# A two-layer encoder trunk: convolution matrices from DRAM, wide convolution, in-place layer norm, reordered start and last head

## The chip, the cores and the metric

The kernel runs on 1 core of one Trainium2 chip. The metric is the device time of one execution in microseconds; a measurement is the median of several runs.

## The reference

The input is x, 1024 frames of 1024 channels, float32. Two layers follow.

- Layer 0: RMS norm; one projection to 1536 columns. 512 "value" columns times the sigmoid of 512 "gate" columns go through a causal depthwise convolution of width 31, a layer norm over the 512 channels, and silu. The other 512 columns are pooled over 2, 4, 8 or 16 past frames, minus the frame itself, and mapped by one 128x128 matrix a group. Both halves are concatenated, projected to 1024 columns and added to x. Then RMS norm, an FFN `(silu(h w1) * (h w3)) w2` with 2816 hidden columns, added.
- Layer 1: RMS norm; a projection to q, f, i, g; a gated linear recurrence of 8 heads with a 128x128 state; head norm times silu(g); output projection, added. RMS norm and an FFN as above. A final RMS norm.

## The kernel before, in words

All activations are transposed: 128 channels by 512 frames is one tile, "half" 0 or 1 of the frames (NH = 2). Every large product is done with operands split into a high and a low part in fp32r, as three matmuls (lines 160 to 162): high times high, low times high, high times low. A weight tile of 128x1024 comes by one DMA on SP's queue into a raw tile (two of these, L141), is cast on ScalarE (L142) and its remainder is taken on VectorE (L143); there are three split tiles of each kind. The residual stream lies in DRAM (`hd`): `accumulate` copies a product out of PSUM into one of three `temp` tiles on ScalarE (L307) and adds it in DRAM by an accumulating DMA from POOL's queue (L308); `fetch` reads it back, also from POOL's queue (L312). `staged` takes a tile out of a pool of 72.

The order of each engine's queue comes from a scheduler that takes the ready instruction of highest priority; `tc.high_priority(offset=...)` lifts a block, `tc.issue_after` puts a block behind one instruction of its engine.

The start (L417 to 441) loads x in 16 tiles, squares it for the row norm (`squares`, ScalarE), transposes it on TensorE (L367), scales and splits it (`keep`), copies it for the residual (`hold`), and makes the first gated product (`glu`). The convolution of channel groups 0, 1 and 2 runs on VectorE, 31 taps of 128x512 each per group and half (`conv`, L470). Group 3 goes to TensorE as 36 products with banded 128x128 matrices (`conv_by_phase`); these matrices are built on GpSimd from a small table of taps and a diagonal (`conv_blocks`, L506), 8 at a time, and the results travel over DMAs (`cb<-cy`) to ScalarE (L539), which writes the group's `y`. Between them run the pooled columns: `project_u`, `map_u` (its copies `v` are L583), `mean_u` (L593), and the pooled half of the output projection (`op`). Then comes the layer norm, half 0 and half 1 (`mu`, `lss`, `ly`), and the convolved half of the output projection (`oa`) with its residual adds (L329).

In layer 1, `recur` is one head and half of the recurrence; it yields between its steps, and after each yield the loop takes that many steps (`BEFORE`) of a "filler": the projections of the next head (`project`: F, Q, values, and the gate G), then the output product of finished heads where `OUT_AT` says so (`ho`). One step is three matmuls of 512 columns, or as much. Behind the last head follows the rest of the output product with the residual (`h_ho`). An FFN starts with two column blocks done together, whose row norms are spread over the partitions by `rows`: a diagonal (`dg`, L200, VectorE) times ones on TensorE (`bc`).

Of the kernel before, what the change touches and what calls it, by code (L numbers as in the profile page):

```python
# [39 lines left out]
def trunk(ctx: ExitStack, tc: tile.TileContext, a, out):  # L40
# [94 lines left out]
    def load(src, shape, leng=None):  # L135
        uid[0] += 1
        i, n = uid[0], shape[0] * shape[1]
        raw = wpool.tile([P, 1024], F32, tag="wraw", name=f"wr{i}", bufs=NRAW)[:, :n]
        wh = wpool.tile([P, 1024], F32R, tag="wh", name=f"wh{i}", bufs=NSPLIT)[:, :n]
        wl = wpool.tile([P, 1024], F32R, tag="wl", name=f"wl{i}", bufs=NSPLIT)[:, :n]  # L140
        nc.sync.dma_start(out=raw.rearrange("p (a b) -> p a b", a=shape[0]), in_=src)  # L141
# [3 lines left out]
        return v(wh), v(wl)  # L145

    def cols(w, m0, nm=1, k0=0, nk=None):
# [3 lines left out]
    last_product = []  # L151
# [18 lines left out]
    def split(src, name, scale=None):  # L170
        hi, lo = act(f"{name}h"), act(f"{name}l")
        if scale is None:
            nc.scalar.copy(hi, src)
            nc.vector.tensor_tensor(lo, src, f32(hi), ALU.subtract)  # L174
        else:
            nc.scalar.activation(hi, src, AF.Copy, scale=scale)
# [14 lines left out]
    def broadcast(y, name, room, bank=mbank):  # L191
# [6 lines left out]
        for i, v in enumerate((f32(yh), yl)):  # L198
            dg = room(f"dg{i}_{name}").bitcast(F32R)
            nc.vector.tensor_tensor(dg.rearrange("p (t q) -> p t q", q=P), ident.unsqueeze(1).to_broadcast([P, 4, P]),  # L200
# [4 lines left out]
    class Norm:  # L205
# [39 lines left out]
        def rows(self, hf, y, bank=mbank):  # L245

            ps = broadcast(y, f"{self.name}{hf}", staged, bank)
# [56 lines left out]
    def accumulate(k, hf, ps, name):  # L304

        o = temp(f"ev_{name}{k}_{hf}")
# [28 lines left out]
    def layer0_mixer(norm_next):  # L335
        with tc.tile_pool(name="m0", bufs=2, reuse_waits="tile") as pool:
# [3 lines left out]
            def load_x(hf):  # L340
                xt = []
# [75 lines left out]
            with tc.high_priority(offset=2 * HI):  # L417
# [32 lines left out]
            band = pool.tile([P, 2, NC4, P], F32, name="band", bufs=1)  # L450
            nc.sync.dma_start(out=band, in_=a["c_band"].rearrange("p (b g t) -> p b g t", b=2, t=P))
# [3 lines left out]
            ybuf = [[staged(f"y{c}_{hf}") for hf in range(NH)] for c in range(NC4)]  # L455
            for y in sum(ybuf[:NC4 - 1], []):
# [16 lines left out]
            traw = pool.tile([P, PH * PS * PH], F32, name="traw", bufs=1)  # L473
            nc.sync.dma_start(out=traw, in_=a["conv_taps"])
            taps = [pool.tile([P, PH * PS * PH], F32, name=f"taps{z}", bufs=1) for z in "hl"]
            nc.scalar.copy(taps[0].bitcast(F32R), traw)
            nc.vector.tensor_tensor(taps[1], traw, taps[0], ALU.subtract)
            diag = pool.tile([P, PG], F32, name="diag", bufs=1)
            nc.vector.tensor_tensor(diag, ident[:, :PG], ident[:, PG:2 * PG], ALU.add)
            for r in range(2, PH):  # L480
                nc.vector.tensor_tensor(diag, diag, ident[:, r * PG:(r + 1) * PG], ALU.add)
# [18 lines left out]
            def conv_blocks(i, n):  # L500

                uid[0] += 1
                w = []
                for t, z in zip(taps, "hl"):
                    m = wpool.tile([P, 1024], F32R, tag=f"w{z}", name=f"cw{z}{i}", bufs=NSPLIT)[:, :n * P]
                    nc.gpsimd.tensor_tensor(  # L506
                        m.rearrange("p (a b) -> p a b", b=PG), diag.unsqueeze(1).to_broadcast([P, n * PH, PG]),
                        t[:, i * PH:(i + n) * PH].unsqueeze(2).to_broadcast([P, n * PH, PG]), ALU.mult)
                    w.append(m.rearrange("p (a b) -> p a b", b=P))
                return w  # L510

            def conv_by_phase(c, xq):
                bp = [staged(f"cb{i}") for i in range(2)]
                for i in range(PH * PS):
# [18 lines left out]
                    if i % 8 == 7:  # L533
                        yield
                for i in range(2):
# [5 lines left out]
                yield  # L541
# [7 lines left out]
            for hf in range(NH):  # L549
                conv(0, hf)  # L550
            project_a(1)
            for hf in range(NH):
                conv(1, hf)
            project_a(NC4 - 1)

            with tc.high_priority(offset=HI):
# [6 lines left out]
                def project_u(g, hf):  # L563
                    if hf == 0:
                        wu = load(*cols(w_in, 8 + g))
                        wp = pool.tile([P, P], F32, tag="wp", name=f"wp{g}", bufs=2)
# [20 lines left out]
                def mean_u(g, hf):  # L587
                    v = vs[g, hf]
                    ps = mbank(f"um{g}_{hf}")
                    for t in range(4):  # L590
                        first = hf == 0 and t == 0
                        o = ps[:, t * P:(t + 1) * P]
                        nc.tensor.matmul(o, v[:, t * P:(t + 1) * P], band[:, 0 if first else 1, g], start=True, stop=first)  # L593
# [18 lines left out]
                for m2 in range(4):  # L612
                    wo = load(*cols(w_out, 2 * m2, 2, 4, 4))
                    for mo in range(2):
                        for hf in range(NH):
                            po = gbank(f"op{m2}_{mo}_{hf}")
                            gemm(po, wo, mo, ps_[hf])
# [634 lines left out]
```

## Time and profile before

| | before |
|---|---|
| runs, us | 2322.33, 2321.64, 2317.51 (median 2321.64) |
| profiled execution, us | 2319.05 |
| its span, us | 2317.2 |
| mean granted TensorE clock | 0.983 |
| TensorE busy | 2233.5 us, 96% |
| TensorE weight loads busy | 1873.9 us, 81% |
| VectorE busy | 1566.5 us, 68% |
| ScalarE busy | 836.7 us, 36% |
| GpSimd busy | 330.1 us, 14% |

Busy time is the union of an engine's instructions. Matmuls are pipelined, so two that follow each other overlap in the record, and a busy TensorE is not one at its peak. The clock is given as a share of 2.4 GHz; it has two levels, 1.2 and 2.4 GHz, and a mean between 0.5 and 1 says which part of a stretch was spent at the lower one. A wait is put down to the instruction whose end came last before it ended.

### The profile page before, as it was taken

How to read it: one execution, taken by the hardware profiler on the slowest of the kernel's cores; microseconds unless marked ns; L12 is line 12 of the kernel's file. 1: busy time of each engine (PE TensorE's matmuls, PEld its weight loads, DVE VectorE, ACT ScalarE, POOL GpSimd, SP SyncE). 2: the span in 40 equal slices, each digit the busy share in tenths (PEclk: the TensorE clock that was granted, in tenths of full speed). 3: DMA queues.
4: the chain of work that ended last, by engine and by line, in shares of the span. 5: the costliest groups of instructions: out<-in, count | busy, mean ns of one | idle time of the engine just before them, and what ended most of it. 6: DMA issues, size and time to landing. Idle time of an engine off the chain costs nothing.

```text
span 2317.2 us, 28669 instructions
## 1 busy us (share of the span) xinstructions
PE 2233.5 (96%) x10814; PEld 1873.9 (81%) x10814; DVE 1566.5 (68%) x2924; ACT 836.7 (36%) x1354; POOL 330.1 (14%) x341
## 2 busy tenths in 40 slices
PE   7998999999999999999999899988899999999998
PEld 6887777888888888888888789876688888888877
DVE  6999695738373736858887387866956464737377
ACT  5223654333333333532222322234543333323336
POOL 1030334010101010310000200035220101010110
PEclk9998999999999999999999999998999999999999
DMA  7103735161515252631111611176153434242544
GB/s 230 56 11 80 186 116 109 55 127 55 117 54 113 62 111 71 210 100 37 46 46 37 118 37 47 37 140 188 55 109 91 91 86 96 74 99 73 100 136 155
DMA packets 220746, 218.18 MB, mean 94 GB/s; under 512 B 9332, under 2 KB 181568, under 8 KB 220608
## 3 DMA queue, kind: packets, MB, share of 16 engines
q1 hardware_dynamic: 186320, 130.18, 18.5%
q0 software_dynamic: 27008, 73.41, 17.1%
q10 hardware_dynamic: 7280, 12.76, 1.5%
q8 instruction: 85, 1.39, 0.2%
q14 instruction: 53, 0.43, 0.1%
HBM read 137.67 MB, written 77.59 MB: 93 GB/s over the span
## 4 chain that ended last, share of the span: by engine, by line
PE 56%; issue 25%; DVE 9%; POOL 2%; DMA 2%; ACT 1%; SPq 0%; ACTq 0%; POOLq 0%; DVEq 0%
PE f1o L160 3%; PE f1o L161 3%; PE f1o L162 3%; PE f0o L161 3%; PE f0o L162 3%; PE f0o L160 3%; DVE y L470 3%; POOL hd L308 1%; DVE wl L143 1%; PE op L160 1%; PE op L161 1%; PE op L162 1%; PE f_5p L735 1%; PE f_18p L735 1%; PE f_18p L733 1%
## 5 line engine op out<-in xcount | busy, mean ns | idle before, releaser
L143 DVE TENSOR_TENSOR wl<-wr,wh 128x1024 fp32r<-128x1024 f32 x130 | 161.4, 1241 | 108.4 <-ACT wh L142 107.7
L142 ACT CAST wh<-wr 128x1024 fp32r<-128x1024 f32 x132 | 138.5, 1051 | 147.1 <-PE pg L161 19.3
L470 DVE SCALAR_TENSOR_TENSOR y<-a,dww,y 128x512 f32<-128x512 f32 x180 | 137.1, 810 | 0.4
L308 POOL DMA_DIRECT2D hd<-ev_ho x40 | 34.8, 892 | 542.0 <-ACT ev_ho L307 534.4
L1029 DVE COPY_PREDICATED S<-masks,pl 128x128 f32<-128x128 uint8 x288 | 92.2, 341 | 13.2 <-PE pl L1011 12.0
L160 PE MATMUL f1o<-f1g_1h,wh 128*128 128x512 f32 (+1 forms) x208 | 74.6, 359 | 1.9 <-ACT f1ev L858 1.9
L1011 PE MATMUL pl<-M,K 128*128 128x192 f32 x384 | 73.0, 334 | 3.5 <-DVE M L998 3.5
L161 PE MATMUL f1o<-f1g_1l,wh 128*128 128x512 f32 (+1 forms) x208 | 74.1, 356 | 0.0
L162 PE MATMUL f1o<-f1g_1h,wl 128*128 128x512 f32 (+1 forms) x208 | 74.1, 356 | 0.0
L160 PE MATMUL f1o<-f1g_0h,wh 128*128 128x512 f32 x176 | 69.3, 393 | 4.2 <-DVE f_0u L762 2.9
L160 PE MATMUL f0o<-f0g_0h,wh 128*128 128x512 f32 x176 | 69.2, 393 | 2.4 <-DVE f_0u L762 2.4
L1011 PEld LDWEIGHTS pl<-M,K 128*128 128x128 f32 x384 | 65.5, 194 | 6.9 <-ACT M L1001 2.2
L161 PE MATMUL f1o<-f1g_0l,wh 128*128 128x512 f32 x176 | 69.5, 395 | 1.1 <-DVE f1g_0l L174 1.1
L160 PE MATMUL f0o<-f0g_1h,wh 128*128 128x512 f32 x176 | 68.6, 390 | 1.4 <-ACT f0ev L858 1.4
L162 PE MATMUL f1o<-f1g_0h,wl 128*128 128x512 f32 x176 | 69.1, 392 | 0.4 <-DVE wl L143 0.4
L162 PE MATMUL f0o<-f0g_0h,wl 128*128 128x512 f32 x176 | 69.2, 393 | 0.0
L161 PE MATMUL f0o<-f0g_0l,wh 128*128 128x512 f32 x176 | 69.1, 393 | 0.0
L161 PE MATMUL f0o<-f0g_1l,wh 128*128 128x512 f32 x176 | 68.6, 390 | 0.1
L162 PE MATMUL f0o<-f0g_1h,wl 128*128 128x512 f32 x176 | 68.5, 389 | 0.0
L864 ACT COPY f1ev<-f1o 128x512 f32<-128x512 f32 x64 | 37.4, 585 | 80.1 <-PE f1o L162 66.1
L864 ACT COPY f0ev<-f0o 128x512 f32<-128x512 f32 x64 | 37.4, 585 | 78.7 <-PE f0o L162 67.2
L866 POOL DMA_DIRECT2D hd<-f0ev x32 | 27.8, 869 | 219.6 <-ACT f0ev L864 217.3
(5437 smaller groups left out, 7075.6 us busy)
## 6 DMA issues: line engine op xcount, KB each, us to landing
wr<-in_ffn_w SPq DMA_DIRECT2D x56, 512.0 KB, 3.4
wr<-in_hg_w_in SPq DMA_DIRECT2D x40, 512.0 KB, 4.0
hd<-f0ev POOLq DMA_DIRECT2D x32, 512.0 KB, 5.1
hd<-f1ev POOLq DMA_DIRECT2D x32, 512.0 KB, 5.2
hd<-ev_ho POOLq DMA_DIRECT2D x40, 256.0 KB, 5.2
h_f<-hd POOLq DMA_DIRECT2D x32, 256.0 KB, 5.4
wr<-in_cp_w_in SPq DMA_DIRECT2D x12, 512.0 KB, 4.2
wr<-in_cp_w_out SPq DMA_DIRECT2D x12, 512.0 KB, 3.6
```

What stands on the lines that cost most here:

```text
L142: nc.scalar.copy(wh, raw)
L143: (leng or nc.vector).tensor_tensor(wl, raw, f32(wh), ALU.subtract)
L160: nc.tensor.matmul(ps, lh, xh, start=k == 0, stop=False)
L161: nc.tensor.matmul(ps, lh, xl, start=False, stop=False)
L162: mm = nc.tensor.matmul(ps, ll, xh, start=False, stop=k == len(xs) - 1)
L308: nc.gpsimd.dma_start(out=hd[k][:, half(hf)], in_=o, accum_op=ALU.add)
L470: nc.vector.scalar_tensor_tensor(acc, tap(at, j, t0, n), dww[:, j, c:c + 1], acc, ALU.mult, ALU.add)
L735: mm = nc.tensor.matmul(ps, wl[:, k], xh, start=False, stop=k == len(xs) - 1)
L864: nc.scalar.copy(os[i][:, half(hf)], product(mg, i, hf, w))
L866: nc.gpsimd.dma_start(out=hd[mg + i], in_=os[i], accum_op=ALU.add)
L1011: nc.tensor.matmul(pl[:, c], K[:, ch[cc]], M[:, :, cc * 64:(cc + 1) * 64], start=True, stop=True)
L1029: nc.vector.copy_predicated(sv, mk.unsqueeze(1).to_broadcast([P, 2, 64 // w, w]), pl[:, :, j, :].rearrange("p c (b n) -> p c b n", n=w))
```

## The change

Loading a weight tile is cut in two calls, the DMA and the split. The x tiles are loaded by column half first. At the start the squares of half 0 and the split of the second weight tile are put behind the copies of half 0. The convolution matrices of group 3 are laid out whole on the host and come as five weight tiles from DRAM; the building on GpSimd goes. The convolution of groups 0 and 1 runs over 1024 frames at once, but for the first 8 taps of group 0. The last copies of group 3 move behind the pooled columns. The layer norm writes into its own tiles; the pooled output product stands between its halves; four residual tiles are fetched early from SP's queue. The diagonals of the FFN's row norms go to GpSimd. In layer 1 a head's gate projection becomes filler of its own head, and the output product of heads 0 and 1 is cut: half 0 behind head 4, half 1 in the last head, whose evictions take `staged` tiles and whose recurrence takes more filler at each yield.

```diff
     def broadcast(y, name, room, bank=mbank, eng=nc.vector):
...
-            nc.vector.tensor_tensor(dg.rearrange("p (t q) -> p t q", q=P), ...
+            eng.tensor_tensor(dg.rearrange("p (t q) -> p t q", q=P), ...
...
-    def accumulate(k, hf, ps, name):
-        o = temp(f"ev_{name}{k}_{hf}")
+    def accumulate(k, hf, ps, name, room=temp):
+        o = room(f"ev_{name}{k}_{hf}")
...
-    def fetch(k, hf, name):
+    def fetch(k, hf, name, eng=nc.gpsimd):
         h = staged(f"h_{name}{k}_{hf}")
-        nc.gpsimd.dma_start(out=h, in_=hd[k][:, half(hf)])
+        eng.dma_start(out=h, in_=hd[k][:, half(hf)])
...
             def load_x(hf):
-                for t in range(4):
-                    xt.append([staged(f"x{hf}_{t}_{i}") for i in range(2)])
-                    for i in range(2):
+                for i in range(2):
+                    for t in range(4):
+                        xt[t][i] = staged(f"x{hf}_{t}_{i}")
...
-                v0 = squares(0, x0)
                 pend = [(0, k, transpose_in(0, x0, k, gbank if 3 < k < 7 else mbank)) for k in range(KT)]
-                wg = load(*cols(w_in, 4), leng=nc.gpsimd)
-                x1 = load_x(1)
+                wr, x1 = fetch_weights(*cols(w_in, 4)), load_x(1)
                 for p in pend[:7]:
                     keep(*p)
-                hold(*pend[0])
+                with tc.issue_after(last_cast[0]):
+                    hold(*pend[0])
                 keep(*pend[7])
                 for p in pend[1:]:
                     hold(*p)
+                with tc.issue_after(last_cast[0]):
+                    wg = split_weights(*wr, leng=nc.gpsimd)
+                    v0 = squares(0, x0)
...
-            def conv(c, hf):
-                acc, at, t0, n = ybuf[c][hf], ats[c], hf * H, H
-                for j in range(CW):
+            def conv(c, hf=None, taps=range(CW)):
+                at = ats[c]
+                acc, t0, n = (ywide[c], 0, T) if hf is None else (ybuf[c][hf], hf * H, H)
+                for j in taps:
...
             def conv_blocks(i, n):
-                for t, z in zip(taps, "hl"):
-                    m = wpool.tile([P, 1024], F32R, tag=f"w{z}", name=f"cw{z}{i}", bufs=NSPLIT)[:, :n * P]
-                    nc.gpsimd.tensor_tensor(...
+                return load(a["conv_taps"][:, i * P:(i + n) * P].rearrange("p (a b) -> p a b", b=P), (n, P))
...
             for hf in range(NH):
-                conv(0, hf)
+                conv(0, hf, range(8))
+            conv(0, taps=range(8, CW))
             project_a(1)
-            for hf in range(NH):
-                conv(1, hf)
+            conv(1)
...
-                for m2 in range(4):
-                    wo = load(*cols(w_out, 2 * m2, 2, 4, 4))
...
+                for _ in cbp:
+                    pass
...
                     for c in range(NC4):
-                        t = staged(f"ly{hf}_{c}")
-                        nc.vector.tensor_tensor(t, ybuf[c][hf], bc, ALU.mult)
+                        t = ybuf[c][hf]
+                        nc.vector.tensor_tensor(t, t, bc, ALU.mult)
...
+            layer_norm(0)
+            pooled_out(range(4))
             ahead = Ahead("oa", [(k, hf) for hf in range(NH) for k in range(KT)])
+            with tc.high_priority(offset=HI):
+                for k in range(4):
+                    ahead.got[k, 0] = fetch(k, 0, "oa", nc.sync)
+            layer_norm(1)
...
-                    rs[hf] = norm.rows(hf, ys[hf], gbank)
+                    rs[hf] = norm.rows(hf, ys[hf], gbank, nc.gpsimd)
...
-        OUT_AT = {3: (([0, 1], (0, 1)),), 7: (([2, 3], (0, 1)), ([4, 5], (0,)))}
+        OUT_AT = {4: (([0, 1], (0,)),), 7: (([0, 1], (1,)), ([2, 3], (0, 1)), ([4, 5], (0,)))}
+        BEFORE_LAST = {0: 8, 2: 5, 4: 6, 6: 5, "k": 5, "S": 4, "o": 3, "T": 10}
...
-        def filler(hd, tiles):
+        def filler(hd, tiles, G):
+            yield from output_gate(hd, G)
             if hd + 1 < HEADS:
                 yield from project(hd + 1, tiles)
             for hds, halves in OUT_AT.get(hd, ()):
-                yield from project_out(hds, halves)
+                yield from project_out(hds, halves, late=hd + 1 == HEADS)
```

`output_gate` is the part of `project` from L964 to L972, moved out. `pooled_out` is the loop from L612 to L618. The band matrices move from a pool tile into two `staged` ones.

## Rows read from the trace of the kernel before

**Rows 1.** Windows by stage; columns stand in the first line
```profile
core 0: us, PE busy (x) PEld busy (x) DVE busy (x) ACT busy (x) POOL busy (x), PEclk, DMA share, GB/s
8.20:51.60 43.40, 36.09 (x164) 29.27 (x164) 31.97 (x66) 28.55 (x61) 4.70 (x14) 0.92 0.71 237
51.60:148.00 96.40, 96.26 (x462) 80.77 (x461) 95.80 (x146) 18.45 (x32) 8.97 (x5) 1.00 0.17 50
148.00:197.00 49.00, 46.69 (x299) 42.05 (x298) 49.00 (x64) 15.20 (x33) 12.42 (x6) 0.97 0.09 29
197.00:258.50 61.50, 53.99 (x235) 44.03 (x234) 48.49 (x89) 28.96 (x48) 13.19 (x15) 0.89 0.62 127
258.50:310.30 51.80, 46.90 (x196) 37.97 (x195) 40.00 (x50) 28.16 (x42) 24.04 (x27) 0.93 0.66 205
1035.00:1285.00 250.00, 250.00 (x1522) 222.22 (x1521) 200.06 (x592) 71.32 (x148) 0.00 (x0) 1.00 0.15 43
1285.00:1320.00 35.00, 29.57 (x149) 23.82 (x147) 6.54 (x8) 13.25 (x22) 13.89 (x16) 1.00 0.85 142
1504.00:1574.60 70.60, 61.28 (x309) 50.78 (x307) 43.45 (x130) 26.96 (x51) 22.09 (x27) 0.95 0.76 140
1574.60:1617.20 42.60, 32.83 (x120) 25.74 (x121) 31.70 (x36) 19.39 (x29) 25.10 (x24) 0.84 0.65 208
```

**Rows 2.** Timeline of the start, all engines: start, duration, instruction, idle before
```profile
8.20 5.93 PE L367 MATMUL xT<-ident,x 128*128 128x128 f32 x28
14.32 3.57 ACT L176 ACTIVATE hn_0h<-xT,prm 128x512 fp32r<-128x512 f32 x6
18.39 4.04 DVE L177 SCALAR_TENSOR_TENSOR hn_0l<-xT,prm,hn_0h 128x512 fp32r<-128x512 f32 x6
19.19 0.80 PE L161 MATMUL av<-hn_0l,wh 128*128 128x512 f32 x1 [3.64 <-DVE hn_0l L177]
```

**Rows 3.** Timeline of VectorE and GpSimd in the convolution
```profile
77.05 3.40 DVE L470 SCALAR_TENSOR_TENSOR y<-a,dww,y 128x512 f32<-128x512 f32 x5
...
121.87 8.13 DVE L470 SCALAR_TENSOR_TENSOR y<-a,dww,y 128x512 f32<-128x512 f32 x8
...
123.11 2.37 POOL L506 TENSOR_TENSOR cwl<-diag,tapsl 128x1024 fp32r<-128x1024 f32 x1
```

**Rows 4.** The page's costliest groups: the split of one weight tile
```profile
L143 DVE TENSOR_TENSOR wl<-wr,wh 128x1024 fp32r<-128x1024 f32 x130 | 161.4, 1241 | 108.4 <-ACT wh L142 107.7
```

**Rows 5.** Timeline near 206 us, ScalarE and TensorE
```profile
205.25 1.25 ACT L539 ACTIVATE y<-cb,prm 128x256 f32<-128x256 f32 x2 [6.20 <-DMA cb<-cy]
...
206.68 0.80 PE L593 MATMUL um<-band,v 128*128 128x128 f32 x2 [7.26 <-ACT v L583]
```

**Rows 6.** Timeline and chain of waits near 260 to 275 us
```profile
260.80 2.52 POOL L312 DMA_DIRECT2D h_oa<-hd  x4
...
261.40 9.85 DMA wr<-in_cp_w_out
...
275.11 0.79 PE L160 MATMUL oa<-a_0h,wh 128*128 128x512 f32 x1 [4.65 <-DVE h_oa L329]
```

**Rows 7.** Groups by line, 1285 to 1320 us: the head product behind head 3
```profile
L307 ACT COPY ev_ho<-ho 128x512 f32<-128x512 f32 x16 | 9.4, 587 | 20.3 <-DMA hd<-ev_ho 18.8 <-PE ho L162 1.5
```

**Rows 8.** Waits of 1504 to 1580 us, and the restart after the last head
```profile
ACT ev_ho L307 <- DMA hd<-ev_ho: 18.8, 14, 4.1
...
1579.51 0.79 PE L160 MATMUL ho<-og_0h,wh 128*128 128x512 f32 x1 [5.00 <-DVE h_ho L329]
```

**Rows 9.** The page's DMA issues: the accumulating store of the head product
```profile
hd<-ev_ho POOLq DMA_DIRECT2D x40, 256.0 KB, 5.2
```

**Rows 10.** Timeline of the FFN start: VectorE and GpSimd
```profile
346.85 0.69 DVE L200 TENSOR_TENSOR dg_nf<-ident,yh_nf 128x512 fp32r<-128x512 f32 x1
359.35 1.77 DVE L775 TENSOR_TENSOR f_0c<-f_0c,f_0c 128x512 f32<-128x512 f32 x1
...
358.30 2.27 POOL L774 TENSOR_TENSOR f_1c<-f_1c,bcs_nf 128x512 f32<-128x512 f32 x1
```

More of the change, by code (lines that the diff above doesn't have):

```diff
@@ L449, in layer0_mixer @@
                 nc.gpsimd.tensor_copy(masks[:, i:i + m], mrow.rearrange("p (l t) -> p l t", t=64))
-            band = pool.tile([P, 2, NC4, P], F32, name="band", bufs=1)
-            nc.sync.dma_start(out=band, in_=a["c_band"].rearrange("p (b g t) -> p b g t", b=2, t=P))
+            band = [staged(f"band{b}") for b in range(2)]
+            for b in range(2):
+                nc.sync.dma_start(out=band[b], in_=a["c_band"][:, b * H:(b + 1) * H])
             bprev = pool.tile([P, NC4, 16], F32, name="bprev", bufs=1)
             nc.sync.dma_start(out=bprev, in_=a["c_bprev"].rearrange("p (g t) -> p g t", t=16))
-            ybuf = [[staged(f"y{c}_{hf}") for hf in range(NH)] for c in range(NC4)]
-            for y in sum(ybuf[:NC4 - 1], []):
+            ywide = [pool.tile([P, T], F32, name=f"y{c}", bufs=1) for c in range(2)]
+            ybuf = [[y[:, half(hf)] for hf in range(NH)] for y in ywide]
+            ybuf += [[staged(f"y{c}_{hf}") for hf in range(NH)] for c in range(2, NC4)]
+            for y in ywide + ybuf[2]:
                 nc.gpsimd.memset(y[:, :1], 0.0)
@@ L471, in conv @@
                                                        ALU.mult, ALU.add)
[L473 to L481, printed above, removed]
             CONV_AT, C2_AT = [4, 5, 6, 7, 8], 4
@@ L592, in mean_u @@
                         o = ps[:, t * P:(t + 1) * P]
-                        nc.tensor.matmul(o, v[:, t * P:(t + 1) * P], band[:, 0 if first else 1, g], start=True, stop=first)
+                        nc.tensor.matmul(o, v[:, t * P:(t + 1) * P], band[0 if first else 1][:, g * P:(g + 1) * P], start=True, stop=first)
                         if not first:
@@ L648, in layer0_mixer, with pooled_out @@
                         as_[hf][c] = split(t, f"a{c}_{hf}")
+            def pooled_out(steps):
+                with tc.high_priority(offset=HI):
+                    for m2 in steps:
+                        wo = load(*cols(w_out, 2 * m2, 2, 4, 4))
+                        for mo in range(2):
+                            for hf in range(NH):
+                                po = gbank(f"op{m2}_{mo}_{hf}")
+                                gemm(po, wo, mo, ps_[hf])
+                                accumulate(2 * m2 + mo, hf, po, "op")
+            layer_norm(0)
+            pooled_out(range(4))
             ahead = Ahead("oa", [(k, hf) for hf in range(NH) for k in range(KT)])
+            with tc.high_priority(offset=HI):
+                for k in range(4):
+                    ahead.got[k, 0] = fetch(k, 0, "oa", nc.sync)
+            layer_norm(1)
             for hf in range(NH):
@@ L927, in project @@
         def project(hd, tiles):
-            F, Q, K, G = tiles
+            F, Q, K = tiles
             if hd % 2:
@@ L1094, in hgrn, with project_out @@
         ogs = [[None] * HEADS for _ in range(NH)]
-        def project_out(hds, halves, ahead=None):
+        def project_out(hds, halves, ahead=None, late=False):
             n = len(hds)
@@ L1111, in project_out @@
                         else:
-                            accumulate(mg + mo, hf, po, f"ho{hds[0]}_")
+                            accumulate(mg + mo, hf, po, f"ho{hds[0]}_", staged if late else temp)
         def new_tiles():
-            return [[None] * NH for _ in range(4)]
-        def filler(hd, tiles):
+            return [[None] * NH for _ in range(3)]
+        def filler(hd, tiles, G):
+            yield from output_gate(hd, G)
             if hd + 1 < HEADS:
@@ L1140, in hgrn @@
             for hf in range(NH):
-                for n in recur(hd, hf, late, *(x[hf] for x in pr)):
+                for n in recur(hd, hf, late, G, *(x[hf] for x in pr)):
                     advance(n)
```

75 lines of the change are left out of this document (35 added, 40 removed).

## Prediction

> **What bounds the kernel now.** I first read busy time by stage, with the granted clock beside it. In the FFN, 1698 to 2250 us, [rows 1] TensorE is busy all the time at full clock and does 2437 matmuls in 552 us, 0.2265 us each; nearly all have 512 columns, so this is the price of one. The recurrence, 1035 to 1285, and the convolution, 51.6 to 148, are also full [rows 1]. No matmul of these is taken away, so only the stages where TensorE stands idle or runs at the lower clock can give time. A stage's loss is its window less TensorE's busy time, plus (1 - clock) times the window, since the lower level is half speed; a stall that is itself at the low clock counts twice, so this is a ceiling. By [rows 1]:
> - start, 8.2 to 51.6: 7.3 + 3.5 = 10.8 us;
> - 148 to 197: 2.3 + 1.5 = 3.8 us;
> - pooled product and layer norm, 197 to 258.5: 7.5 + 6.8 = 14.3 us;
> - convolved product, 258.5 to 310.3: 4.9 + 3.6 = 8.5 us;
> - output product behind head 3, 1285 to 1320: 5.4 us;
> - last head, 1504 to 1574.6: 9.3 + 3.5 = 12.8 us; its restart, to 1617.2: 9.8 + 6.8 = 16.6 us.
>
> Then I read what ends the idle time in each, in the timeline and the waits.
>
> **The change part by part.** All sums are against the profiled execution, 2319.05 us; it lies 2.6 us under the median of the three runs, which is 0.1%.
>
> *Start.* The 28 transposes end at 14.13, and the first cast begins only then, because ScalarE squares x first; VectorE's remainders begin at 18.39, behind the row norm, and TensorE's second matmul waits until 19.19 [rows 2]. With the squares behind the copies the casts follow the transposes bank by bank, so the products can start at 14.1: 19.2 - 14.1 = **5 us** earlier. The second weight tile is now split after the copies, about 17 us (from 9, eight casts of 0.6 [rows 2], five copies), and GpSimd's half takes 2.4 us as [rows 3] has it for 1024 elements; ready at 20, before 24 matmuls at the lower clock are through. The eight squares (by the casts' 0.6 some 5 us of ScalarE) now lie ahead of half 1's casts; ScalarE was busy 28.6 of 43.4 us [rows 1], so they fit, but if not the part costs 3. Bounds: 8 better to 3 worse. The x order brings the first four transposes forward by up to four tile loads; the tap transposes in front of them still wait for their own small load, so I give it nothing.
>
> *Convolution.* VectorE: 54 pairs of 512-element taps become 54 of 1024. A tap starts each 0.66 us (five in 3.40, less the tail) [rows 3]; 512 more elements cost 0.55 us (1.24 for 1024 [rows 4], 0.69 for 512 [rows 10]), so about 0.11 us goes per pair, 6 us in all. GpSimd's ten building instructions of 1.6 to 2.4 us go: eight taps took 8.13 us beside two of them and would have taken 5.4 [rows 3], so some 2.7 us for two, 13 us for ten. New are five splits of weights, 1.24 us of VectorE each at most [rows 4], 6 us, and five casts on ScalarE, which is idle for four fifths of that stage. VectorE thus gains about 13 us, but TensorE was full there [rows 1], so directly only the 2.3 us idle of 148 to 197 can go: **2 us** (0 to 4). The five new tiles must pass SP's queue, two raw tiles and three split tiles; a tile takes some 4 us to land and 2.3 to split, and between two blocks TensorE has 24 matmuls (5.4 us) and more, so I cost their waits at nothing while the load is issued a block ahead. What it costs without that cover is the slower rival.
>
> *Pooled product.* TensorE's 7.26 us before 206.68 wait for ScalarE's copy `v`, and that stands behind the two copies of group 3, which wait 6.20 us for a DMA [rows 5]. The copies now stand behind all pooled work, so the wait goes, with some 2 us of low clock after it: **9 us** (0 to 14). What is late next is the layer norm itself. It still waits for those copies, but the pooled product, 192 matmuls or 43 us, runs beside it, and VectorE, busy 48.5 of 61.5 us there [rows 1], comes 13 us less laden, so the first half's norm should end before the product.
>
> *Convolved product.* Here TensorE waits 4.65 us at 275.11 for the residual add, whose tiles were fetched from POOL's queue at 260.80, behind the last accumulating store [rows 6]. Four of them now go on SP's queue earlier, and half 1's norm runs under half 0's product: **4 us** (2 worse to 8 better). The new wait is at the head of SP's queue: a fetch waits for the stores of its channel, and weight tiles queue behind it; two raw tiles cover that for 10 us. Writing the norm in place frees tiles and costs nothing; the same instructions run.
>
> *Output product of heads 0 and 1.* Behind head 3 ScalarE idles 18.8 us for the three eviction tiles that wait for their accumulating stores [rows 7]; a store takes 5.2 us from issue to landing [rows 9]. Sixteen outputs in a row are 96 matmuls, 21.7 us, in a window of 35. After head 4 there are eight, which the three tiles and four PSUM banks nearly absorb: **7 us** (3 to 8.5), the 5.4 idle and the slow matmuls behind it.
>
> *Last head.* A head costs 62.5 us in the recurrence [rows 1], of which 64 steps of three matmuls are 43.5, so its own work is 19. The last head had 144 product matmuls, 32.6 + 19 = 51.6 us, and took 70.6: 19 us are lost, more than the idle time shows, because lone matmuls look long. ScalarE waited 14 times, 18.8 us, for the same three tiles [rows 8], and its copies for the recurrence stood behind. With `staged` tiles this wait goes, and 80 steps instead of 48 fill the recurrence's own latencies: 54.4 + 19 = 73.4 us ideal. The added 32 steps are not new work but taken from heads 0 and 3. I take **16 us** of the 19 (4 to 20). The gate products moved into their own head are the same matmuls; a head's first step now follows Q directly instead of the gate, but needs only half 0's Q, 8 steps (5.4 us) old. The restart after it, 5.00 us for the fetch [rows 8], I leave as it is: as many stores lie before it (4 better to 5 worse).
>
> *FFN diagonals.* Eight of 0.6 us leave VectorE, which is nearly full there. GpSimd's product of that size took 1.3 to 2.3 us, and VectorE's L775 beside it 1.77 for 0.6 [rows 10]: some 1.2 us lost per 2.3 of GpSimd. Saved 8 x 0.6 = 4.8, lost 8 x 1.3 x 0.5 = 5: **0** (3 better to 5 worse).
> The Trainium skill, page "SBUF — State Buffer", section "SBUF: two separate sides", says that VectorE with two SBUF inputs and a GpSimd instruction that reads SBUF lock each other out for a whole instruction; the rows show about half of that, and the fourth rival is what the rule would make of it.
>
> **Sum.** -5 - 2 - 9 - 4 - 7 - 16 + 0 = -43: 2319 - 43 = **2276 us**.
>
> **Rivals.**
> - *DMA bounds the last head.* Its DMA share was already 0.76 with 24 stores [rows 1], and 0.85 behind head 3; now there are 32. The backlog then appears at the restart: 6 instead of 16, and 5 more there: 2291 us. Against it: 32 stores over a longer head are about the same rate. 18%.
> - *The norm chain bounds.* The layer norm goes through VectorE, ScalarE and TensorE in turn; if the second half does not fit under the product, pooled and convolved parts give 4 instead of 13: 2285 us. 12%.
> - *The reordering doesn't take.* The moved parts keep their high priority, and the scheduler may queue the start and the pooled product as before: 5 + 4 lost, 2285 us. 10%.
> - *GpSimd locks VectorE out* in both FFN starts, 8 x 1.3 us lost for 4.8 saved: 6 us, 2282 us. For it: nearly all that VectorE does there reads two operands, and L775 was held [rows 10]; against it: held by 1.2 of 2.3 us. 8%.
> - *Slower: the convolution tiles come late.* If each of the five is issued only when its block is due, it costs a DMA like the 9.85 us in the chain [rows 6], five times: +49, and the sum becomes 2325 us. It decides where a tile lands more than 8.6 us after its block is due, for then five eat the 43. For it: two raw tiles and one SP queue that also carries waits; against: TensorE has 24 or more matmuls between blocks. 5%.
>
> My forecast keeps 47%. The range takes the bounds: all parts at their better ends are 8 + 4 + 14 + 8 + 8.5 + 20 + 7 = 70 us, of which I keep 61 (2258), since not all come together; several rivals together, or one with the lower bounds, leave some 17 (2302). 0.2%, or 4.6 us, is about what a measurement of this kernel can tell from no change. Faster 0.92, same 0.03, slower 0.05, the slower rival.
>
> **What would show it.** The transposes' casts should begin near 9 us and the second matmul of `av` near 14; no wait of `um` for `v`; `op` without a gap until `oa`; no wait of `ho` for `ev_ho`; the last head near 75 us. I am wrong if TensorE waits for `wl` at the `cp` products, if the fetch after the last head takes longer, or if the time saved by 260 us is given back before 360, where VectorE is the bound.

## The result and the profile after

Four runs of the changed kernel give 2291.38, 2288.10, 2287.74 and 2295.47 us, median 2289.74; four of the kernel before have the median 2319.57. The ratio is 0.9877, 95% interval 0.9851 to 0.9902. The profiled execution is the 2291.38 one (span 2289.6, clock 0.989), 27.6 us of span under the one before. The forecast was 2276, the range 2258 to 2302: direction and range hold, 30 of the 43 us came. One of the six runs of e11 below took 2662.99 us at a granted clock of 0.785, and e11's ratio is taken without it.

Windows by stage of the kernel after, cut where its stages begin and end; the columns are those of [rows 1]:

```profile
core 0: us, PE busy (x) PEld busy (x) DVE busy (x) ACT busy (x) POOL busy (x), PEclk, DMA share, GB/s
8.20:49.60 41.40, 36.36 (x159) 27.32 (x158) 31.02 (x68) 29.00 (x63) 4.70 (x10) 0.92 0.74 247
...
146.00:194.90 48.90, 48.90 (x327) 44.78 (x326) 45.71 (x61) 18.99 (x38) 0.00 (x0) 1.00 0.23 69
194.90:240.90 46.00, 45.25 (x199) 36.14 (x199) 37.58 (x66) 25.21 (x41) 13.12 (x15) 1.00 0.80 153
240.90:288.00 47.10, 46.16 (x203) 36.72 (x201) 36.79 (x54) 24.96 (x37) 21.21 (x21) 1.00 0.70 212
288.00:377.90 89.90, 72.85 (x285) 56.20 (x286) 69.29 (x111) 44.38 (x70) 35.90 (x33) 0.91 0.34 80
...
1467.00:1545.30 78.30, 78.01 (x403) 66.11 (x402) 48.92 (x137) 34.77 (x62) 29.90 (x36) 1.00 0.82 159
1545.30:1588.50 43.20, 31.21 (x120) 23.70 (x120) 31.14 (x34) 20.31 (x31) 21.32 (x21) 0.92 0.69 224
```

From the pooled product to the end of the convolved one (194.9 to 288.0) TensorE now stands idle for 1.7 us at full clock, where [rows 1] had 12.4 us idle and a clock of 0.89 to 0.93: both parts did there what they were meant to. Yet the next row is longer than before. From the last `oa` matmul to the first matmul of the third product of FFN 0 (`f_2p`) it takes 89.9 us, against 79.5 in the kernel before, which has no wait there at its beginning:

```profile
310.30:389.80 79.50, 70.30 (x285) 54.34 (x284) 63.92 (x107) 41.50 (x66) 29.19 (x26) 0.94 0.35 77
```

So layer 0 was 22.3 us ahead at 288.0 and 11.9 ahead at `f_2p` (377.9 against 389.8).

The rest: from the first projection of layer 1 (`pf`) to the first FFN 1 product the recurrence takes 612.3 us instead of 628.9; FFN 1's start (to its `f_2p`) 80.8 instead of 80.4, what follows, up to the last matmul, 613.2 instead of 613.5.

The answers to [rows 2, 3, 4, 9], from the timeline of the start, the page's groups and its DMA issues:

```profile
10.17 4.18 ACT L182 ACTIVATE hn_0h<-xT,prm 128x512 fp32r<-128x512 f32 x7 [1.10 <-PE xT L373]
12.76 0.39 PE L167 MATMUL av<-hn_0l,wh 128*128 128x512 f32 x1
...
23.86 0.63 ACT L358 ACTIVATE xq<-x 128x512 f32<-128x512 f32 x1
...
24.47 0.69 ACT L182 ACTIVATE hn_1h<-xT,prm 128x512 fp32r<-128x512 f32 x1
```

```profile
L483 DVE SCALAR_TENSOR_TENSOR y<-a,dww,y 128x512 f32<-128x512 f32 (+1 forms) x127 | 118.1, 968 | 0.7
```

```profile
L146 DVE TENSOR_TENSOR wl<-wr,wh 128x1024 fp32r<-128x1024 f32 x137 | 168.3, 1228 | 109.8 <-ACT wh L145 109.4
```

```profile
hd<-ev_ho POOLq DMA_DIRECT2D x40, 256.0 KB, 7.0
```

The start's second matmul runs at 12.76 instead of 19.19. Half 1's casts wait for the squares, until 24.47, and the pooled columns (`u`) begin at 94.0 instead of 96.0: 2 us are left. The taps take 118.1 us. From the chain of waits of layer 0 (start, duration, what), mostly VectorE's pieces are shown here:

```profile
200.28 4.74 DVE y L483 x8
...
205.51 0.69 DVE ysum L620
206.33 1.10 PE mu L621 x2
...
235.83 1.10 PE mu L621 x2
...
244.92 0.69 DVE h_oa L335
...
286.44 2.31 DVE f_0a1l L713
...
291.99 1.14 DVE f_1a1l L713
293.12 0.66 DVE hn_nf0t_1r L291
293.79 0.72 DVE h_oa L335 x2
```

VectorE leads to the mean of half 0 at 206.33. Then the chain lies on TensorE, in the pooled product and half 1's mean, until the add at 244.92: the three lines of `op` are 25.5% of the answer from 170 to 300 us, the fetches of `h_oa` 7.3%. From 286.44 on, with weight remainders and residual adds, it is VectorE again. So the chain by itself does not say that VectorE's load sets the end of the layer; only the experiments can. At its end stands TensorE's new wait, where the kernel before had none:

```profile
284.75 1.76 DVE L726 TENSOR_TENSOR f_0w<-f_0w 128x512 f32<-128x512 f32 x1 [3.88 <-POOL f_0s L725]
...
293.70 1.27 DVE L335 TENSOR_TENSOR h_oa<-h_oa,oa 128x512 f32<-128x512 f32 x2
...
294.53 0.77 PE L742 MATMUL f_0p<-hn_nf0b_0h,f_0a1h 128*128 128x512 f32 x1 [6.55 <-ACT hn_nf0t_1h L179]
```

The wait is put down to a cast, but that has long ended. `f_0p` needs a PSUM bank, and the adds that free one (293.70) stand in VectorE's queue behind FFN 0's weight sums.

In the recurrence, the waits of 1467 to 1590 us have no `ev_ho` behind a DMA any more ([rows 8] had 14, 18.8 us). Behind head 4, where the evictions still take `temp` tiles, they are there (1262 to 1345), and TensorE waits in head 5; the restart is as before. First that wait (us in total, times, longest), then TensorE's timeline:

```profile
ACT ev_ho L313 <- DMA hd<-ev_ho: 7.8, 4, 4.7
```

```profile
1345.35 2.90 PE L1023 MATMUL pl<-M,K 128*128 128x192 f32 x8 [4.41 <-DVE M L1010]
...
1549.87 0.80 PE L166 MATMUL ho<-og_0h,wh 128*128 128x512 f32 x1 [4.87 <-DVE h_ho L335]
```

### The profile page after: what moved, and what is told of

Read it like the earlier page. It is cut to its first block, busy times and chain, and to the rows that moved or that the text cites. A ratio compares the mean times of both kernels' runs of the same rounds, so it can differ in the third digit from the quotient of the medians.

```text
span 2289.6 us, 28591 instructions
## 1 busy us (share of the span) xinstructions
PE 2222.2 (97%) x10814; PEld 1865.2 (81%) x10814; DVE 1550.5 (68%) x2865; ACT 841.8 (37%) x1360; POOL 313.9 (14%) x333
## 3 DMA queue, kind: packets, MB, share of 16 engines
q10 hardware_dynamic: 7280, 12.76, 1.5%
## 4 chain that ended last, share of the span: by engine, by line
PE 70%; issue 17%; DVE 7%; DMA 3%; ACT 2%; POOL 1%; ACTq 0%; DVEq 0%; POOLq 0%; SPq 0%
PE f0o L166 3%; PE f0o L167 3%; PE f0o L168 3%; PE f1o L166 3%; PE f1o L167 3%; PE f1o L168 3%; PE pl L1023 1%; PE u L166 1%; PE u L168 1%; PE u L167 1%; PE ho L166 1%; PE av L167 1%; PE ag L166 1%; PE ag L167 1%; PE ag L168 1%
## 5 line engine op out<-in xcount | busy, mean ns | idle before, releaser
L146 DVE TENSOR_TENSOR wl<-wr,wh 128x1024 fp32r<-128x1024 f32 x137 | 168.3, 1228 | 109.8 <-ACT wh L145 109.4
L145 ACT CAST wh<-wr 128x1024 fp32r<-128x1024 f32 x139 | 145.4, 1046 | 213.2 <-PE pv L927 28.3
L483 DVE SCALAR_TENSOR_TENSOR y<-a,dww,y 128x512 f32<-128x512 f32 (+1 forms) x127 | 118.1, 968 | 0.7
L1041 DVE COPY_PREDICATED S<-masks,pl 128x128 f32<-128x128 uint8 x288 | 93.7, 340 | 16.2 <-PE pl L1023 15.0
L166 PE MATMUL f0o<-f0g_1h,wh 128*128 128x512 f32 x176 | 69.2, 393 | 2.7 <-ACT f0ev L867 2.7
L167 PE MATMUL f0o<-f0g_1l,wh 128*128 128x512 f32 x176 | 69.2, 393 | 0.0
```

The source lines that it names most:

```text
L166: nc.tensor.matmul(ps, lh, xh, start=k == 0, stop=False)
L167: nc.tensor.matmul(ps, lh, xl, start=False, stop=False)
L483: nc.vector.scalar_tensor_tensor(acc, tap(at, j, t0, n), dww[:, j, c:c + 1], acc, ALU.mult, ALU.add)
L1041: nc.vector.copy_predicated(sv, mk.unsqueeze(1).to_broadcast([P, 2, 64 // w, w]), pl[:, :, j, :].rearrange("p c (b n) -> p c b n", n=w))
```

## The experiments

Runs e1 to e10 are one execution each, beside a run of the kernel before on the same chip (2315.69 to 2318.32 us). The four runs of the changed kernel lie 7.7 us apart, so small differences are read by stage, and these vary too: e3 and e4 have the changed kernel's code in the whole of layer 0, and in the profiles of the three the last `oa` matmul ends at 288.0, 290.1 and 291.8, `f_2p` begins at 377.9, 377.8 and 379.6, and from `f_0p` to `f_2p` it takes 83.3, 80.5 and 81.4. Steadier is the stretch from the first pooled column (`u`) to `f_2p`: 283.9, 283.2 and 283.7.

**e1, the squares last.**

```diff
-                    v0 = squares(0, x0)
...
                     hold(1, k, ps)
+                with tc.issue_after(last_cast[0]):
+                    v0 = squares(0, x0)
```

> The changed kernel with the eight squares of half 0 put behind half 1's copies. Theory: in the changed kernel half 1's first cast begins at 24.5 us because the squares of half 0 hold ScalarE from 18.6 to 24.4, and this gives back most of the 6.8 us that half 0 gained; without them the casts begin near 19, the products of half 1 end 4 us earlier, the first u matmul starts near 90 instead of 94.0, and the whole is 3 to 4 us shorter. Rival: the pace of half 1 is set by the round of cast, remainder and copy over the PSUM banks, or the row norm that now comes later holds the banks; then u starts at 94 or later and the time stays.

2287.37 us. The casts of half 1 begin at 22.2, but `u` at 94.7: TensorE waits 3.57 us at 45.27 for the row norm's diagonal and 1.40 more behind it. So the order of the squares does not decide when the start ends: what one half gains the row norm loses. That ScalarE's load is the bound is not shown, for it is busy 29.0 of the 41.4 us in the changed kernel; in e1 its copies of half 1 wait some 1.5 us each for VectorE's remainder, which is the round that the rival names.

**e2, deeper fetches for `oa`.**

```diff
-            for kk in self.order[:i + 3]:
+            for kk in self.order[:i + (6 if self.name == "oa" else 3)]:
```

> The changed kernel with the residual tiles of the convolved product fetched six ahead instead of three. Theory: the 6.55 us before the first FFN product is a PSUM bank that is free only after the last residual adds at 293.7, whose tiles were fetched at 287.6 behind GpSimd's own work; with deeper fetches the wait falls below 2 us and the FFN start begins 4 to 6 us earlier. Of that, 2 to 5 us should be left at the first product of block 2. Rival: VectorE is the bound from there on; the FFN start begins earlier but is longer by as much, and the first product of block 2 stays at 377.9 within 1 us.

2286.23 us. `f_0p` still waits 5.75 us for an add, and `f_2p` begins at 377.5. The DMA was not what made the adds late.

**e3, staged evictions behind head 4 too.**

```diff
-                yield from project_out(hds, halves, late=hd + 1 == HEADS)
+                yield from project_out(hds, halves, late=True)
```

> The changed kernel with staged tiles for the evictions behind head 4 too. Theory: the 4.41 us wait for M at 1345 comes from three eviction tiles: ScalarE stands 4.75 us before the seventh eviction, the weight cast behind it and VectorE's remainder, which stands 9.87 us, hold up the first products of the recurrence. Without it the wait and the slow matmuls behind go, 5 to 6 us. Rival: the eight stores at once slow the weight tiles on the DMA engines, and the wait is then for a weight tile: 0 to 2 us.

2283.98 us. Head 5 takes 62.4 us, as every undisturbed head, with no wait in it; in the eight profiles where the changed code stands there it took 65.0 to 69.2. The lost time behind head 4 was the three tiles'.

**e4, half 0 of heads 4 and 5 first in the last head.**

```diff
-7: (([0, 1], (1,)), ([2, 3], (0, 1)), ([4, 5], (0,)))}
+7: (([4, 5], (0,)), ([2, 3], (0, 1)), ([0, 1], (1,)))}
```

> The changed kernel with the last head's output products in the order heads 4 and 5 half 0, heads 2 and 3, heads 0 and 1 half 1, so that the last eight stores are all of half 1. Theory: the 4.87 us before the restart is the fetch of half 0, which waits for stores of half 0 that were issued last; now it can be issued earlier and the wait falls to 1 us or less: 3 to 5 us off. Rival: the fetch stands on GpSimd's queue behind the stores whatever half they write, so the wait stays near 5 us and the time is the same.

2293.27 us. The restart waits 4.92 us: this order of the stores does not shorten it.

**e5, the diagonals back on VectorE.**

```diff
-                    rs[hf] = norm.rows(hf, ys[hf], gbank, nc.gpsimd)
+                    rs[hf] = norm.rows(hf, ys[hf], gbank)
```

> The changed kernel with the FFN diagonals back on VectorE. Theory of the prediction: neutral; the two FFN starts (first product to first product of block 2: 83.3 and 80.8 us) change by less than 1.5 us each. Rival, GpSimd locks VectorE out: each start gets about 3 us shorter. Third: the move was a gain, each start gets 1 to 3 us longer.

2284.55 us. From `f_0p` to `f_2p` FFN 0 takes 80.4 us instead of 83.3, FFN 1 80.5 instead of 80.8. The first pair proves little, since e3 has 80.5 with the diagonals on GpSimd; but from the first `u` to `f_2p` e5 takes 280.0 us, against 283.2 to 283.9 in the three profiles above, so 3 to 4 us are gained. On GpSimd the four diagonals of FFN 0 come one after the other, and TensorE waits for two of them, 1.02 and 1.74 us; in e5 it waits for none (after, timeline of GpSimd and TensorE):

```profile
331.90 1.41 POOL L206 TENSOR_TENSOR dg_nf<-ident,yh_nf 128x512 fp32r<-128x512 f32 x1
333.76 2.02 POOL L206 TENSOR_TENSOR dg_nf<-ident,yl_nf 128x512 fp32r<-128x512 f32 x1 [0.45 <-DVE yl_nf L202]
...
335.84 0.54 PE L208 MATMUL bc_nf<-dg_nf,ones 128*128 128x512 f32 x1 [1.74 <-POOL dg_nf L206]
```

**e6, the convolution narrow again** (512 frames a tap), the matrices still from DRAM.

```diff
-                conv(0, hf, range(8))
-            conv(0, taps=range(8, CW))
+                conv(0, hf)
...
-            conv(1)
+            for hf in range(NH):
+                conv(1, hf)
```

> The changed kernel with the convolution of groups 0 and 1 over 512 frames at a time again, 31 taps a half. Theory: TensorE sets the pace until the layer norm, so 6 us more of VectorE cost nothing: the last um matmul stays at 194.9 and the first FFN product at 294.5, within 1.5 us. Rival: VectorE's chain sets the layer norm; the norm's first mu (206.3) and what follows come 4 to 6 us later.

2291.24 us. VectorE's taps by the pages, e6 and below it the kernel before:

```profile
L483 DVE SCALAR_TENSOR_TENSOR y<-a,dww,y 128x512 f32<-128x512 f32 x180 | 125.2, 748 | 0.2
```

```profile
L470 DVE SCALAR_TENSOR_TENSOR y<-a,dww,y 128x512 f32<-128x512 f32 x180 | 137.1, 810 | 0.4
```

So GpSimd's building cost the taps 11.9 us, and the width saves 7.1 more (118.1). `u` (93.7) and the first `mu` (205.0) come no later than in the changed kernel (94.0 and 206.3), as "costs nothing" has it, but the last `oa` matmul ends at 297.3, against 288.0 to 291.8, and from the first `u` to `f_2p` it takes 287.3 us, against 283.2 to 283.9. So 3 to 4 of VectorE's 7.1 us reach the end of the layer, behind every window in which TensorE is full.

**e7, the kernel before with staged evictions** for the products that `OUT_AT` names, and nothing else.

```diff
...
-        o = temp(f"ev_{name}{k}_{hf}")
+        o = room(f"ev_{name}{k}_{hf}")
...
-                            accumulate(mg + mo, hf, po, f"ho{hds[0]}_")
+                            accumulate(mg + mo, hf, po, f"ho{hds[0]}_", staged if late else temp)
...
-                yield from project_out(hds, halves)
+                yield from project_out(hds, halves, late=True)
```

> The kernel before, with staged tiles for the evictions of the output product behind head 3 and in the last head, and nothing else. Theory: three eviction tiles were the cause in both stages: 6 to 8 us less behind head 3 and 8 to 11 of the 13.5 lost in the last head. Rival: in the last head the recurrence's own latencies are the cause, which need the 32 added steps: there at most 4 us less, some 11 in all.

2295.03 us against 2318.32 on the same chip. Head 3 with its product takes 84.4 us, which is a plain head (62.4) and 96 matmuls (21.7); head 4 takes 62.3. The last head and its restart take 96.1 us instead of 113.3, which is more than the 8 to 11 expected (e8, with the old code there, took 110.3). ScalarE's waits from 1210 to 1640 us (columns as above) name no store for `ev_ho`; this is the one row of it:

```profile
ACT ev_ho L307 <- PE ho L162: 23.1, 24, 1.7
```

The recurrence takes 605.1 us, less than the 612.3 of the changed kernel's profile. The kind of tile alone gives all that the recurrence gained.

**e8, the kernel before with the last copies moved** behind the pooled columns.

```diff
+                yield
                 for i in range(2):
...
-                yield
...
+                for _ in cbp:
+                    pass
```

> The kernel before, with only the last copies of group 3 moved behind the pooled columns. Theory: the 7.26 us wait of TensorE for v goes, with 2 us of low clock: the last um matmul ends near 201 instead of 210.7, and the first FFN product comes 6 to 9 us earlier than 310.2. Rival: the norm waits for the same copies, so product and norm only change places: um ends earlier, but the first FFN product moves by less than 2 us.

2318.25 us. The pooled columns end 5.9 us earlier and the pooled product 4.7, but then `oa` waits 9.33 us at 275.54 for a residual add and ends at 310.7, as before. Nothing is gained.

**e9, residual adds ahead of FFN 0's sums** in VectorE's queue, tiles fetched six ahead.

```diff
+                        with sooner(1000) if hf else nullcontext():
+                            h = ahead(2 * m2 + mo, hf)
...
-                nc.vector.tensor_tensor(a2[:, 0], a2[:, 0], a2[:, 1], ALU.add)
+                with tc.issue_after(last_add[0]) if self.first else nullcontext():
+                    nc.vector.tensor_tensor(a2[:, 0], a2[:, 0], a2[:, 1], ALU.add)
```

> The last residual adds of half 1 are put ahead of FFN 0's weight sums in VectorE's queue (the sums stand behind the last add), and their tiles are fetched six ahead; nothing else. Theory: the 6.55 us that TensorE waits ahead of the first f_0p at 294.53 come from VectorE's order (an in-order queue whose head waits 3.88 us for GpSimd's f_0s, with four residual adds behind it that hold PSUM banks). Then f_0p begins within 2 us of the last oa matmul, by 290, and the third product of FFN 0 (f_2p) begins 3 to 6 us earlier than 377.9; span 3 to 6 us below 2289.6. Rival: VectorE is simply full from 250 to 380 us, so what is moved ahead only moves something else behind: f_0p begins earlier, but f_2p stays within 1.5 us of 377.9.

2294.53 us. `f_0p` follows the last `oa` matmul without a wait (290.3), so, with the fetches alone ruled out by e2, the wait was VectorE's order. But `f_2p` begins at 378.7: TensorE now waits 0.99, 2.31 and 1.12 us for remainders that came later. The rival held: the wait moved. (The edit also stands in FFN 1, whose start took 91.6 us instead of 80.8, so the whole time says nothing of layer 0.)

**e10, remainders of the convolution tiles on GpSimd.**

```diff
-                return load(a["conv_taps"][:, i * P:(i + n) * P].rearrange("p (a b) -> p a b", b=P), (n, P))
+                return load(a["conv_taps"][:, i * P:(i + n) * P].rearrange("p (a b) -> p a b", b=P), (n, P), nc.gpsimd)
```

> The remainders of the five convolution tiles are taken on GpSimd instead of VectorE. Theory: from the wide convolution to the end of the convolved product it is VectorE's chain (taps, norm of half 0, norm of half 1, adds) that sets the end, so five times 1.22 us less, half of it given back beside GpSimd, bring the first mu matmul (206.3) and the last oa matmul (288.0) 2 to 5 us forward. Rival: TensorE's own work sets them: mu comes forward, but the last oa matmul stays within 1 us. Slower rival: GpSimd's 2.4 us for a remainder come later than VectorE's 1.2, the cp products wait, and um ends later than 194.9.

2283.30 us. None of the readings fits well. The taps take 127.0 us, 8.9 more, beside five GpSimd instructions of 1.6 to 4.6 us, which outweighs the five remainders (8.9 against 5.6 us), so VectorE is not relieved; `um` ends at 198.8 instead of 194.9, as the slower rival has it, the last `oa` matmul at 290.2. Yet `f_2p` begins at 373.7, 4.2 us earlier, and 280.2 us behind the first `u`. Half 1's norm sum begins earlier too, at 230.3 instead of 233.6. Of these 3.3 us, 1.9 are a wait of VectorE for ScalarE's cast in half 0's norm (`a_0h`), 0.31 us where the changed kernel has 2.23.

**e11, the kernel before with two edits**: the convolution (from DRAM, wide, norm in place) and the staged tiles.

```diff
+                return load(a["conv_taps"][:, i * P:(i + n) * P].rearrange("p (a b) -> p a b", b=P), (n, P))
...
+            conv(0, taps=range(8, CW))
...
+            conv(1)
...
+                yield from project_out(hds, halves, late=True)
```

> The kernel before with two edits of the change alone: (1) the convolution (matrices from DRAM, groups 0 and 1 over 1024 frames, norm in place), (2) staged eviction tiles for the output products of finished heads. Left out: the x order and the start's order, the moved copies, the pooled product between the norms, the early fetches, GpSimd's diagonals, the moved gate, the moved products, the longer filler. Theory: these two carry the whole gain, since layer 0 ends by VectorE's chain, which begins with the end of the convolution's taps, and the recurrence lost its time to three eviction tiles. Then the last tap ends 9 to 12 us before 229.9, the first f_2p of FFN 0 begins within 2 us of 377.9, the last head and its restart take 94 to 98 us instead of 112.7, and the time is 2281 to 2288 (ratio 0.983 to 0.987), no more than after's. Rival: the reordering of TensorE's and ScalarE's work carries layer 0; then f_2p stays at 384 to 390 and the time is that of the staged tiles alone, 2291 to 2296 (0.988 to 0.991).

Median 2284.20 us, ratio 0.9848 (0.9836 to 0.9861). The theory held but for the last tap, which ends 8.2 us earlier than before instead of the 9 to 12 named: `f_2p` is at 379.3, last head and restart take 95.8 us. Two parts of the change give all of its gain; by the medians they give 5 us more, though the intervals (0.9836 to 0.9861, 0.9851 to 0.9902) just overlap.

**e12, the changed kernel with the edits of e3, e5 and e10.**

```diff
+                yield from project_out(hds, halves, late=True)
...
+                    rs[hf] = norm.rows(hf, ys[hf], gbank)
...
+                return load(a["conv_taps"][:, i * P:(i + n) * P].rearrange("p (a b) -> p a b", b=P), (n, P), nc.gpsimd)
```

> The kernel after with three edits that gained in single runs: remainders of the convolution tiles on GpSimd, FFN diagonals on VectorE, staged evictions behind head 4 too. If they add up: 4 us (f_2p at 373.7 instead of 377.9), 3 us in FFN 0's start and 5 us behind head 4, so 2275 to 2281 (ratio 0.981 to 0.984), below after's 0.9877. If the first two relieve the same VectorE chain and only one of them counts, 2280 to 2284 (0.984 to 0.986). If single runs misled, 2287 to 2291 as after.

Median 2281.39 us, ratio 0.9837 (0.9825 to 0.9850). `f_2p` begins at 375.4, as with e5 alone (375.3): e5 and e10 do not add up, and head 5 takes 62.4 us. It lies just below the changed kernel's interval; from e11 the intervals don't part it.

## Why the prediction came out as it did

The range held in part by luck. Layer 0 gave 11.9 us of 20 and the recurrence 16.6 of 23 (7 + 16), and several of the parts came out otherwise than reasoned.

**Layer 0: 20 us forecast, 12 measured.** The step that failed is the one on the convolution: "VectorE thus gains about 13 us, but TensorE was full there [rows 1], so directly only the 2.3 us idle of 148 to 197 can go", and with it the habit of adding start, pooled and convolved product as gaps of TensorE. At the last `oa` matmul the gaps had given 22.3 us: 2.0 in the start (5 forecast; the rest was lost within it), 0.1 up to the pooled stage (2), 15.5 in the pooled stage (9) and 4.7 in the convolved one (4). Before `f_2p` 10.4 us of these came back, as the 6.55 us wait and the slower FFN start. The terms under the convolution were good: VectorE's taps shed 19.0 us (137.1 to 118.1; forecast 6 + 13) and five remainders cost 5.9 (group of `wl` from 45 to 232 us: 16.7 to 22.6 us), which leaves 13.1. What e11 shows is that the edits of the convolution and its norm, for which the sum saw 2.3 us of idle time, bring `f_2p` forward by 10.5 us without the other parts. The milestones, in us:

| profile | last tap ends | half 1's `ysum` begins | last `oa` ends | first `f_2p` | first `u` to `f_2p` |
|---|---|---|---|---|---|
| before | 229.9 | 246.0 | 310.3 | 389.8 | 293.8 |
| e8 | 231.1 | 248.0 | 310.7 | 390.6 | 294.4 |
| e6 | 227.4 | 237.3 | 297.3 | 381.0 | 287.3 |
| e11 | 221.6 | 233.6 | 296.8 | 379.3 | 283.2 |
| after | 218.4 | 233.6 | 288.0 | 377.9 | 283.9 |
| e4 | 222.4 | 237.6 | 291.8 | 379.6 | 283.7 |
| e9 | 220.9 | 236.1 | 290.5 | 378.7 | 285.4 |
| e5 | 219.7 | 234.9 | 289.2 | 375.3 | 280.0 |
| e10 | 216.6 | 230.3 | 290.2 | 373.7 | 280.2 |

`f_2p` follows half 1's norm sum by 140.4 to 145.7 us in all fourteen profiles (e1, e5 and e12 the shortest), while from the last `oa` matmul it varies from 79.5 to 90.3. The start, the moved copies, the pooled product between the norms and the early fetches bring the end of `oa` forward by 5.0 to 8.8 us (e11 to after and e4) and `f_2p` by no more than 1.4; behind the first `u` nothing of them is left. The prediction's last condition ("given back before 360, where VectorE is the bound") named this; the second rival named a chain too, but in the product instead of behind it.

That the convolution's gain arrives through VectorE's load is argued and not shown. For it: e6 gives VectorE 7.1 us more and loses 3 to 4. Against it: in e10 VectorE is busier and `f_2p` comes earlier. The norm in place, which is part of e11, and the freed GpSimd were not run alone.

**FFN diagonals: 0 forecast, 3 to 4 us lost in FFN 0** (e5, from the first `u`), within the bounds. The sum traded busy time against busy time and counted no wait. That the row of four on GpSimd (1.4 to 2.0 us each) is what costs is not shown: with the diagonals on VectorE, TensorE waits for one of them too, 1.62 us in the kernel before and 3.14 in e11.

**Output product of heads 0 and 1: 7 forecast, 2.8 measured.** The price of a matmul, 0.2265 us, is that of the FFN in the kernel before; the prediction names [rows 1] for it, where this row does not stand (columns as there):

```profile
1698.00:2250.00 552.00, 552.00 (x2437) 457.23 (x2436) 313.34 (x440) 180.87 (x256) 62.05 (x69) 1.00 0.40 93
```

Over a plain head (62.4) and the products' own matmuls, before lost 5.8 us in head 3 and 3.8 in head 4; after loses 6.8 in head 5, and 2.6 to 6.8 over the eight profiles with this code, so that up to 7.0 were gained in some. "After head 4 there are eight, which the three tiles and four PSUM banks nearly absorb" is what failed: the loss moved to the next head (4.41 us at 1345.35 and slow matmuls), and e3 takes it away.

**Last head and restart: 16 forecast, 13.2 measured** (113.3 before; 121.8 after, less 96 added matmuls or 21.7 us, is 100.1). The mechanism was right: no eviction waits, TensorE idle for 0.3 us of 78.3. The "19 us lost" was too large, since 24 of the 168 `ho` matmuls in that window belong to the restart; 13.5 is what it held. The staged tiles alone gain 17.2 (e7) and 17.5 (e11), by 96.1 and 95.8 us against the 100.1. So the moved products and the longer filler give some 4 back, at the restart: its window is 43.2 us with 4.87 us of wait, where e11's longest wait is 2.90. The kernel before took 42.6 there, but at a clock of 0.84. In the last head the 32 stores land in 7.7 us (median), the 24 of e11 in 5.8, so the DMA rival may have been there in kind, at under half of its price. That is a comparison of two orders; which of their parts costs it was not tried alone.

**The other rivals.** The reordering took. The convolution's tiles came in time: from 146.0 to 194.9 TensorE is never idle. That GpSimd locks VectorE out was measured by e6 and e10: 21.5 us of GpSimd's building (L506 from 45 to 232 us, groups of 11.5 and 10.0) cost the taps 11.9 us, and 13.9 us of remainders cost 8.9, 0.55 and 0.64 us for each. That is near the half that the prediction took, but VectorE is not held by half. The loss lies in few taps: nine in the kernel before take 1.5 to 2.4 us and the other 171 some 0.74; in e10 five do, one beside each GpSimd instruction (e10, timeline of GpSimd and VectorE; a tap of this width alone takes 1.27):

```profile
150.35 2.38 POOL L146 TENSOR_TENSOR wl<-wr,wh 128x1024 fp32r<-128x1024 f32 x1 [9.52 <-ACT wh L145]
...
150.71 3.10 DVE L483 SCALAR_TENSOR_TENSOR y<-a,dww,y 128x1024 f32<-128x1024 f32 x1
...
154.19 1.27 DVE L483 SCALAR_TENSOR_TENSOR y<-a,dww,y 128x1024 f32<-128x1024 f32 x1
```

This tap ends 1.08 us behind GpSimd's instruction, so it did most of its work only then. The rest of GpSimd's recorded time is its own waiting for VectorE: the same instruction takes 2.35 us in the start, and 4.64 at 116.41 in e10, where the taps at 115.96 and 117.16 still run at full speed and the one at 118.70 takes 3.43. So the prediction misread [rows 10]: GpSimd's 2.27 us at 358.30 hold a wait for VectorE's remainder, which ran to 359.42, and L775 then waited to GpSimd's end (kernel before, timeline of VectorE and GpSimd):

```profile
357.42 2.00 DVE L143 TENSOR_TENSOR wl<-wr,wh 128x1024 fp32r<-128x1024 f32 x1
...
357.05 1.30 POOL L774 TENSOR_TENSOR f_0c<-f_0c,bcs_nf 128x512 f32<-128x512 f32 x1 [35.06 <-DVE f_0c L757]
```

The Trainium skill, page "SBUF — State Buffer", section "SBUF: two separate sides", has it as a lock in which "the other fully blocks"; these rows agree with it.

**What stays open** is why e10 gains: VectorE was busier, not less busy. The shorter wait in half 0's norm accounts for 1.9 of the 3.3 us by which its half 1's norm sum comes earlier, and what shortened it is not shown; with e5's edit beside it in e12 the gain is not seen (half 1's norm sum begins at 234.9 there).

## What to carry to other kernels

A stage in which TensorE is full hides another engine's work only until the next stage that waits for that engine: follow each engine's work to the place where it is handed over before costing its savings at nothing (10.5 us came here where 2.3 us of idle time had been counted, e11). An in-order engine that evicts into a small ring filled by slow stores holds up everything queued behind it; a deeper ring was worth 23 us here (e7), and no reordering came near it. Where several edits serve one stage, time them alone: two parts did all the work here, and the rest gave nothing beyond them.

## What the runs showed of the hardware

The same 256 KB accumulating store lands in 5.2 us in the last head when three tiles throttle it, in 5.8 (e11) and 6.0 (e7) when the same 24 stores have tiles of their own, and in 7.7 when there are 32 (medians of the stage's DMA issues): removing the throttle lengthens each store, and yet the whole gets shorter. GpSimd and VectorE, each with two inputs in SBUF, take turns by whole instructions: a tap of 1.27 us beside GpSimd's remainder took 3.10, and a remainder that takes GpSimd 2.35 us in the start took 2.38 to 4.64 beside the taps (e10), because it waits as well. The share of GpSimd's recorded time that VectorE loses (0.55 and 0.64 here) is therefore no measure of how much they overlap.
